# The first group's output projection, three of four head pairs: seven block products for eight

## The chip, the cores and the metric

The kernel runs on one core of a Trainium2 chip. The metric is the device time of one execution in microseconds. Several engines work side by side on a core and wait for one another through semaphores: TensorE (PE: matmuls; PEld is its loading of weights), VectorE (DVE), ScalarE (ACT), GpSimd (POOL); SyncE (SP) issues almost all transfers (DMA).

## What is computed

One layer of a decoder with two kinds of recurrent heads, for 2048 prompt tokens and 64 sample tokens at once. The part that matters here is the projection of the eight heads' outputs back to the model's width of 1024 and its addition to the residual:

```python
def mixer(h, pos, s_ret, s_hg, w_in, ...):
    proj = h @ w_in                          # 1024 -> 4096, cut into q, k, v, gates of 4 + 4 heads
    ...                                      # chunkwise recurrences, a norm per head, a swish gate
    o = jnp.concatenate([o_r, o_h], axis=-1) # 4 retention heads and 4 HGRN2 heads of 128
    return o @ w_out, s_ret_new, s_hg_new    # 1024 x 1024

xp = xp + mp                                 # mp: what mixer gave; the same for the samples
xp = xp + jnp.square(jax.nn.relu(rmsnorm(xp) @ w_up)) @ w_down
```

## The kernel before

**Tiling.** Tokens lie along the free dimension, features along the 128 partitions. They are cut into three groups (`GROUPS`) of 640, 768 and 704 tokens; the 64 samples are the first columns of the third, the rest are prompt tokens. For each group in turn the kernel makes the input norm (`norm_in`), the mixing (`mix`) and the output projection (`out_proj`); then for each group the feed forward (`ffn`), whose products are already made by a scheme of seven for eight.

**Numbers in two parts.** Every factor of a large product is split into `hi` (a rounded copy, made by ScalarE, L271 for weights and L349 for activations) and `lo` (the rest, made by VectorE, L285 and L350). A product is three matmuls: hi x hi, hi x lo, lo x hi. A matmul multiplies a 128 x 128 block of weights with at most 512 columns; a group of 640 tokens is done in two pieces of 320.

**Weights.** `w` lies in memory as tiles of 128 x 1024, eight blocks each, in the order of use. `plan_stream` writes that order; `weight` (L245) loads a tile through one of three `raw` buffers, and splits it into one of three `hi` and three `lo` buffers two tiles ahead of its use. The first group also stores the split parts of tiles 4 to 35 (`next_weight`, L319: 28 of the input projection and four of the output projection); the later groups load them back ("p" entries, L254) and split only the rest ("w"). Sums of weights for the feed forward are made beside the mixing of the second and third group by `plan_sums`, with four further buffers.

**Order.** The code is written in the order of TensorE's work. `tick` counts it: one tick for two matmuls of a projection. `later(n, f)` lets `f` emit its instructions n ticks on, so that side work is laid between matmuls. A scheduler then places the instructions on the engines' queues, in about the order in which they were emitted; each engine and SP work through their queues in order.

**Mixing.** Heads go in four pairs (one head of each kind). For each pair: the gates of the pair before, five projections, a long chain of recurrence work emitted by ticks (`mixer`), the values. After the fourth pair's values, `cut_heads` (L1178) splits the first three pairs' outputs at 2, 20 and 38 ticks, beside the last gates. The fourth pair's own chain ends later, beside the output projection, and `mixer` has its outputs cut then.

**Output projection.** `residual` (L1194) takes the eight output blocks in the order `N_ORDER`. For each it multiplies the six heads of three pairs (`proj`, L331; the matmuls are on L342): 6 x 3 x 2 = 36 matmuls, and adds the x block to the result out of PSUM (L1204). It uses six tiles of weights. After the second block `beside` starts `norm_in` of the next group at 12 ticks a piece: each of its eight pieces loads an x block into one of six `ld` buffers, and gives ScalarE two and VectorE two instructions (L546, L527, L547, L530). Then `out_proj` (L1240) waits until the fourth pair is cut, and adds its part for each block (12 matmuls, L1249), scales by the next norm's weight (L1250) and stores both (L1252). The last two tiles of weights belong to this.

## Time and profile before

| | |
|---|---|
| median of 3 runs | 2508.93 us (2508.18 to 2508.98) |
| the profiled execution, its own time | 2508.95 us |
| its span from the first to the last instruction | 2507.2 us |
| granted TensorE clock | 0.999 |
| first group's last gates begin | 273.5 us into the span |
| its projection of three pairs begins | 294.7 us |
| its fourth pair's part begins, ends | 348.1 us, 362.4 us |

Times within the profile count from the span's first instruction. "Busy" is time in which an engine executes; an engine can be busy less than the whole time and still be the one that others wait for in one stage. A line such as L1204 is that of the kernel's file; `out<-in` names the tiles written and read.

### The profile page before, as it was taken

To read this page: it belongs to the slowest core of one execution; us is meant where nothing else is said; L and a number is where in the kernel's file an instruction comes from. 1 tells how busy PE (TensorE), PEld (TensorE's weight loads), DVE (VectorE), ACT (ScalarE), POOL (GpSimd) and SP (SyncE) were. 2 spreads that over 40 slices of the span, in tenths; PEclk is the share of its full clock that TensorE was granted. 3 is DMA by queue.
4 is the path that set the end of the run, shared out by engine and by line. 5 is a ranking of instruction groups with operands and counts; after the bars stand their busy time and mean duration, and the time that the engine had idled before them with its cause. 6 is when DMAs were issued, how large, how long until landed. Compare 5 with 4: busy or idle time off the path is not lost.

```text
span 2507.2 us, 41510 instructions
## 1 busy us (share of the span) xinstructions
PE 2494.0 (99%) x16593; PEld 2474.9 (99%) x16593; DVE 1878.1 (75%) x2443; ACT 1253.9 (50%) x1674; POOL 366.1 (15%) x304
## 2 busy tenths in 40 slices
PE   9999999999999999999999999999999999999998
PEld 9999999999999999999999999999999999999998
DVE  7666865668684766677775899775699878678987
ACT  6665653444463444443644555444454436445544
POOL 5223304324411432340000000000000000000000
PEclk9999999999999999999999999999999999999999
DMA  7454563465575565758866856566675546867552
GB/s 269 164 185 168 209 225 135 160 228 185 199 244 212 194 215 195 264 206 306 305 216 213 284 198 213 173 237 221 202 261 177 189 148 202 274 192 247 192 187 88
DMA packets 189073, 525.39 MB, mean 210 GB/s; under 512 B 18640, under 2 KB 59856, under 8 KB 188880
## 3 DMA queue, kind: packets, MB, share of 16 engines
q1 hardware_dynamic: 188736, 522.73, 60.6%
q8 instruction: 130, 2.13, 0.3%
q14 instruction: 63, 0.52, 0.1%
q10 hardware_dynamic: 144, 0.02, 0.0%
HBM read 389.50 MB, written 132.38 MB: 208 GB/s over the span
## 4 chain that ended last, share of the span: by engine, by line
PE 96%; DVE 3%; ACT 1%; issue 1%; DMA 0%; DVEq 0%; ACTq 0%
PE pj L342 27%; PE pf L1189 26%; PE pj L1189 25%; PE pjv L732 8%; PE mm L898 1%; PE po L1078 1%; PE mm L1086 1%; PE po L1080 1%; PE mm L955 1%; PE mm L509 1%; PE mm L510 1%; PE mm L1012 1%; PE mm L830 0%; PE po L764 0%; DVE raw L1221 0%
## 5 line engine op out<-in xcount | busy, mean ns | idle before, releaser
L271 ACT CAST hi<-raw 128x1024 fp32r<-128x1024 f32 x392 | 413.1, 1054 | 610.0 <-PE pf L1189 261.4
L342 PE MATMUL pj<-slab,hi 128*128 128x320 f32 (+2 forms) x3072 | 661.5, 328 | 2.6 <-DVE slab L644 1.3
L1189 PE MATMUL pf<-slab,hi 128*128 128x320 f32 (+2 forms) x2768 | 659.1, 321 | 0.0
L1189 PE MATMUL pj<-slab,hi 128*128 128x352 f32 (+2 forms) x2608 | 622.1, 322 | 0.0
L285 DVE TENSOR_TENSOR lo<-raw,hi 128x1024 fp32r<-128x1024 f32 x392 | 485.3, 1238 | 111.9 <-ACT hi L271 105.8
L342 PEld LDWEIGHTS pj<-slab,hi 128*128 128x128 f32 x3072 | 508.1, 188 | 5.3 <-DVE slab L644 1.5
L1189 PEld LDWEIGHTS pf<-slab,hi 128*128 128x128 f32 x2768 | 481.9, 188 | 0.0
L1189 PEld LDWEIGHTS pj<-slab,hi 128*128 128x128 f32 x2608 | 454.5, 188 | 0.1
L1189 PE MATMUL pf<-slab,lo 128*128 128x320 f32 (+2 forms) x1384 | 445.5, 322 | 0.0
L1189 PE MATMUL pj<-slab,lo 128*128 128x352 f32 (+2 forms) x1304 | 420.3, 322 | 0.0
L342 PE MATMUL pj<-slab,lo 128*128 128x320 f32 (+2 forms) x1536 | 379.1, 328 | 0.4 <-DVE lo L285 0.4
L342 PEld LDWEIGHTS pj<-slab,lo 128*128 128x128 f32 x1536 | 263.3, 188 | 1.3 <-DVE lo L285 0.9
L1189 PEld LDWEIGHTS pf<-slab,lo 128*128 128x128 f32 x1384 | 260.3, 188 | 0.0
L1189 PEld LDWEIGHTS pj<-slab,lo 128*128 128x128 f32 x1304 | 245.3, 188 | 0.0
L732 PE MATMUL pjv<-hi,slab 128*128 128x256 f32 x1088 | 204.8, 285 | 0.0
L1280 ACT CAST slab<-slab 128x640 fp32r<-128x640 f32 (+2 forms) x192 | 145.7, 780 | 65.8 <-DVE slab L1291 52.2
L1284 DVE TENSOR_TENSOR slab<-slab 128x640 fp32r<-128x640 f32 (+2 forms) x192 | 167.3, 886 | 8.9 <-PE pj L1189 3.2
L732 PEld LDWEIGHTS pjv<-hi,slab 128*128 128x128 f32 x1088 | 172.2, 192 | 1.5 <-issue 0.2
L732 PE MATMUL pjv<-lo,slab 128*128 128x256 f32 x544 | 153.8, 283 | 0.0
L879 ACT ACTIVATE slab<-slab 128x640 f32<-128x640 f32 (+2 forms) x72 | 56.4, 784 | 154.6 <-POOL slab L875 154.4
L732 PEld LDWEIGHTS pjv<-lo,slab 128*128 128x128 f32 x544 | 104.2, 192 | 0.0
L1536 DVE TENSOR_TENSOR slab<-pf,slab 128x640 f32<-128x640 f32 (+2 forms) x88 | 77.6, 888 | 29.6 <-PE pf L1189 29.1
(218 smaller groups left out, 3004.1 us busy)
## 6 DMA issues: line engine op xcount, KB each, us to landing
raw<-w SPq DMA_DIRECT2D x264, 512.0 KB, 4.2
slab<-u SPq DMA_DIRECT2D x32, 384.0 KB, 4.7
u<-ld SPq DMA_DIRECT2D x30, 384.0 KB, 3.7
slab<-u SPq DMA_DIRECT2D x32, 352.0 KB, 4.5
u<-ld SPq DMA_DIRECT2D x30, 352.0 KB, 4.0
slab<-u SPq DMA_DIRECT2D x32, 320.0 KB, 4.5
u<-ld SPq DMA_DIRECT2D x30, 320.0 KB, 3.9
ld<-x SPq DMA_DIRECT2D x16, 384.0 KB, 3.6
```

The lines of the kernel that those rows point to most:

```text
L271: self.nc.scalar.copy(hi, raw)
L285: self.nc.vector.tensor_tensor(out=lo, in0=self.second.pop(j), in1=hi.bitcast(F32), op=ALU.subtract)
L342: self.nc.tensor.matmul(pj[:, i, :T2], w, a[:, c0:c1], start=j == 0 and q == 0, stop=j == n - 1 and q == 2)
L509: self.nc.tensor.matmul(ps, self.ones_r, hi, start=True, stop=False)
L510: self.nc.tensor.matmul(ps, self.ones_r, lo, start=False, stop=True)
L732: nc.tensor.matmul(pj[:, i * 256:(i + 1) * 256], a[:, s:s + C], ww, start=kb == 0 and q == 0, stop=kb == KB - 1 and q == 2)
L879: nc.scalar.activation(x["dd", w][:, a:T], x["dd", w][:, a:T], AF.Exp)
L898: nc.tensor.matmul(ps[:, j * P:(j + 1) * P], qk[:, cols[c]], qk[:, cols[c]], start=True, stop=True)
L1189: self.nc.tensor.matmul(*a, **k)
L1280: self.nc.scalar.copy(hi[:, :g.T], B[name][:, :g.T])
L1284: self.nc.vector.tensor_tensor(out=lo[:, :g.T], in0=B[name][:, :g.T], in1=hi.bitcast(F32)[:, :g.T], op=ALU.subtract)
L1536: nc.vector.tensor_tensor(out=r, in0=ps, in1=r, op=ALU.add)
```

## The change

For the first group alone (`OUT_SEVEN = (0,)`), the projection of the first three pairs is made by seven products for eight, in two quads t of four output blocks. In a quad the weights are a 2 x 2 arrangement A11, A12, A21, A22 (rows: the two halves of its four output blocks; columns: the HGRN2 and the retention heads), the activations B11, B12 (HGRN2 heads, first and second half of the tokens) and B21, B22 (retention heads). Sums S1 to S4 of weights and T1 to T4 of activations are multiplied, and the results added to four accumulators of a quad, and to a common term U that three of them get at the end.

* The order of the output projection's weights changes for all groups: eight tiles of 768 columns (one kind of head, two output blocks, three pairs), and two tiles of 1024 for the fourth pair. `N_OUT` goes from 8 to 10. `weight`, `second_part` and the kept copies handle the narrower tiles.
* `plan_sums` makes S1 to S4 for both quads beside the first group's mixing, starting at 400 and 592 ticks, and stores them; the products load them from there. A11 and A12 are the tiles that are kept for the later groups.
* `head_sums` replaces the three `cut_heads` of the first group: pairs 0 and 1 at 60 and 130 ticks of the fourth round of mixing, pair 2 beside the last gates.
* `out_seven` makes the 14 products in two PSUM buffers in turn. x is added to a quarter where its first product leaves PSUM. `norm_in` of the second group now starts after the sixth product, at 10 ticks a piece.
* `last_pair` adds the fourth pair by quarters.
* The second and third group's `residual` takes blocks in plain order, two tiles for two blocks.

The core of the diff:

```diff
-N_IN, N_OUT, N_UP, N_DN = 32, 8, 32, 32
+N_IN, N_OUT, N_UP, N_DN = 32, 10, 32, 32
-N_KEPT = W_OUT0 + 4
+WO = 2 * (H - 1) * P
-N_ORDER = (0, 1, 4, 5, 2, 3, 6, 7)
+OUT_SEVEN = (0,)
+OUT_PRODUCTS = ((0, "S4"), (0, "A11"), (1, "A11"), (0, "A12"), (1, "A12"), (1, "S4")) + tuple(
+    (t, name) for t in range(2) for name in ("S3", "S2", "A22", "S1"))
...
+        def mixing(g):
+            self.stream += [("p" if j >= N_MADE and g else "w", j, WT, j >= N_MADE and not g) for j in range(W_OUT0)]
+            products = OUT_PRODUCTS if g in OUT_SEVEN else [(t, name) for t in range(2) for name in ("A11", "A12", "A21", "A22")]
+            for t, name in products:
+                kept = name in ("A11", "A12")
+                e = entry(name, ("o", t), W_OUT0 + 4 * t, WO, kept and not g)
+                self.stream.append(("p",) + e[1:] if kept and g else e)
+            self.stream += [("w", W_UQ0 - 2 + j, WT, False) for j in range(2)]
...
+            self.plan_sums([(("o", t), W_OUT0 + 4 * t) for t in range(2)], [400, 592], WO)
             self.mix(gs[0])
-            self.out_proj(gs[0], 1, lambda: self.norm_in(gs[1], pace=12))
+            self.out_proj(gs[0], 1, lambda: self.norm_in(gs[1], pace=10))
...
+            if p == H - 1 and g.i in OUT_SEVEN:
+                g.ob = {name: [None] * (H - 1) for name in ("B11", "T1", "B21", "B22", "T2", "T3", "T4")}
+                for i in range(2):
+                    self.later(60 + 70 * i, self.head_sums, g, i)
...
+    def head_sums(self, g, p):
...
+        for d, fn, *a in ((0, keep, s, "B21", "B22"), (2, inner), (4, keep, o, "B11", "T1"), (8, outer),
+                          (11, keep, t, "T3", "T2"), (14, last)):
+            self.later(d, fn, *a)
...
+    def out_seven(self, g, beside):
...
+        def product(ps, op, first=True):
+            hi, lo = self.next_weight()
+            for i in range(2):
+                for p in range(H - 1):
+                    cols = slice((i * (H - 1) + p) * P, (i * (H - 1) + p + 1) * P)
...
+                    for j, (w, a) in enumerate(((hi, ah), (hi, al), (lo, ah))):
+                        self.matmul(ps[:, i], w[:, cols], a, start=first and p == 0 and j == 0,
+                                    stop=p == H - 2 and j == 2, skip_group_check=not first)
...
+        x(0, (0, 1))
+        x(0, (0, 0))
+        x(1, (0, 0))
+        x(1, (0, 1))
+        product(a, "B22")
+        new(0, (0, 1), a)
+        product(b, "B11")
+        for t, ps in ((0, b), (1, a)):
+            if t:
+                product(a, "B11")
+            acc[t]["U"] = self.get()
+            nc.scalar.copy(b2(acc[t]["U"]), ps)
+        for t, ps in ((0, b), (1, a)):
+            product(ps, "B21", False)
+            new(t, (0, 0), ps)
+            x(t, (1, 1))
+            x(t, (1, 0))
+        product(b, "B22")
+        new(1, (0, 1), b)
+        beside()
+        for t in range(2):
+            product(a, "T3")
+            new(t, (1, 1), a)
+            product(b, "T2")
+            add(acc[t]["U"], b, acc[t]["U"])
+            product(a, "T4", False)
+            new(t, (1, 0), a)
+            product(b, "T1")
+            add(acc[t][1, 1], b, acc[t][1, 1])
+            add(acc[t][0, 1], b, acc[t][0, 1])
+            for k, q in enumerate(((0, 1), (1, 1), (1, 0))):
+                self.later(4 + 8 * k, common, t, q)
...
     def residual(self, g, when, beside):
...
+        for m in range(KB // 2):
+            w = [self.next_weight(), self.next_weight()]
+            for i in range(2):
```

More of the change, by code (lines that the diff above doesn't have):

```diff
@@ L170, in lay_out_weights @@
     wo = w_out.reshape(2, H, P, KB, P)
-    for ps in (range(0, H - 1), range(H - 1, H)):
-        bl = [wo[kind, p, :, n] for n in N_ORDER for p in ps for kind in (1, 0)]
-        for j in range(0, len(bl), 8):
-            w[i] = np.stack(bl[j:j + 8], 1).reshape(P, WT)
+    for n in range(0, KB, 2):
+        for kind in (1, 0):
+            w[i, :, :WO] = wo[kind, :H - 1, :, n:n + 2].transpose(1, 2, 0, 3).reshape(P, WO)
+            w[i, :, WO:] = 0
             i += 1
+    for n in range(0, KB, 4):
+        w[i] = wo[::-1, H - 1, :, n:n + 4].transpose(1, 2, 0, 3).reshape(P, WT)
+        i += 1
     wu = w_up.reshape(2, KB // 2, P, NQ, 2, 2, P)
@@ L253, in weight @@
                 for part, kept in zip(self.wts[j], self.kept[e[1]]):
-                    self.nc.sync.dma_start(part.bitcast(F32), kept)
+                    self.nc.sync.dma_start(part[:, :e[2]].bitcast(F32), kept)
                 self.w_next += 1
@@ L257, in weight @@
                 continue
-            while self.w_load <= j or j >= W_UQ0 and self.w_load <= j + 2 and self.w_load < n:
+            while self.w_load <= j or j >= self.n_first and self.w_load <= j + 2 and self.w_load < n:
                 if self.stream[self.w_load][0] == "p":
@@ L265, in weight @@
                 e = self.stream[k]
-                self.fetch(raw, self.sums[e[1]] if e[0] == "s" else self.I["w"][e[1]])
+                self.fetch(raw[:, :e[2]], self.sums[e[1]] if e[0] == "s" else self.I["w"][e[1]][:, :e[2]])
                 self.w_load += 1
@@ L270, in weight @@
             lo = self.wp.tile([P, WT], F32R, tag="lo", name="lo")
-            self.nc.scalar.copy(hi, raw)
+            w = self.stream[j][2]
+            self.nc.scalar.copy(hi[:, :w], raw[:, :w])
             self.wts[j] = (hi, lo)
@@ L283, in second_part, with entry @@
         if j in self.second:
-            hi, lo = self.wts[j]
-            self.nc.vector.tensor_tensor(out=lo, in0=self.second.pop(j), in1=hi.bitcast(F32), op=ALU.subtract)
+            (hi, lo), w = self.wts[j], self.stream[j][2]
+            self.nc.vector.tensor_tensor(out=lo[:, :w], in0=self.second.pop(j)[:, :w], in1=hi[:, :w].bitcast(F32), op=ALU.subtract)
     def plan_stream(self):
-        self.stream = [("w", j) for j in range(W_UQ0)]
-        def entry(name, key, i0):
-            return ("s", key + (name,)) if name[0] == "S" else ("w", i0 + A_PLACE[name])
-        def mixing():
-            self.stream += [("p" if N_MADE <= j < N_KEPT else "w", j) for j in range(W_UQ0)]
+        self.stream = []
+        def entry(name, key, i0, cols=WT, keep=False):
+            return ("s", key + (name,), cols, False) if name[0] == "S" else ("w", i0 + A_PLACE[name], cols, keep)
+        def mixing(g):
[6 more added lines that the diff above has]
+            self.stream += [("w", W_UQ0 - 2 + j, WT, False) for j in range(2)]
         def feed_forward():
@@ L302, in feed_forward @@
                     self.stream += [entry(name, ("d", o, v), W_DQ0 + 4 * (2 * o + v)) for v in range(2)]
-        mixing()
-        mixing()
+        mixing(0)
+        self.n_first = len(self.stream)
+        mixing(1)
+        mixing(2)
         self.n_sums = len(self.stream)
@@ L315, in next_weight @@
         r = self.weight(i)
-        if N_MADE <= i < N_KEPT:
-            self.kept[i] = [self.dp.tile([P, WT], F32, name=f"w{i}{part}") for part in ("hi", "lo")]
-            for part, kept in zip(r, self.kept[i]):
-                self.nc.sync.dma_start(kept, part.bitcast(F32))
+        _, j, cols, keep = self.stream[i]
+        if keep:
+            self.kept[j] = [self.dp.tile([P, cols], F32, name=f"w{j}{part}") for part in ("hi", "lo")]
+            for part, kept in zip(r, self.kept[j]):
+                self.nc.sync.dma_start(kept, part[:, :cols].bitcast(F32))
         self.wts.pop(i - 4, None)
@@ L634, in mix @@
             prev = b
-        for p in range(H - 1):
-            self.later(2 + 18 * p, self.cut_heads, g, p)
+        if g.i in OUT_SEVEN:
+            self.later(2, self.head_sums, g, H - 2)
+        else:
+            for p in range(H - 1):
+                self.later(2 + 18 * p, self.cut_heads, g, p)
         self.gates(g, prev)
@@ L1192, in matmul, with keep, inner, outer @@
             self.tick()
+    def head_sums(self, g, p):
+        nc, T, T2 = self.nc, g.T, g.T // 2
+        o, s = g.o[p][1], g.o[p][0]
+        first, second = (lambda t: t[:, :T2]), (lambda t: t[:, T2:T])
+        t, t4 = self.get(), self.get()
+        sub = lambda out, a, b, op=ALU.subtract: nc.vector.tensor_tensor(out=out, in0=a, in1=b, op=op)
+        def keep(slab, *names):
+            hi, lo = self.getr(), self.getr()
+            self.cut(slab, hi, lo, T)
+            for name, half in zip(names, (first, second)):
+                g.ob[name][p] = (half(hi), half(lo))
+        def inner():
+            sub(first(t), second(s), second(o))
+            sub(second(o), second(o), first(o))
+        def outer():
+            sub(second(t), first(t), first(o), ALU.add)
+            sub(first(t4), first(s), second(t))
+        def last():
+            g.ob["T4"][p] = self.parts(first(t4), T2)
+        for d, fn, *a in ((0, keep, s, "B21", "B22"), (2, inner), (4, keep, o, "B11", "T1"), (8, outer),
+                          (11, keep, t, "T3", "T2"), (14, last)):
+            self.later(d, fn, *a)
@@ new lines, in rows, with x, add, common @@
+    def rows(self, g, name, n, c0, c1):
+        s = self.load()
+        o = KB * g.off
+        src = self.I["x"][:, o:o + KB * g.T].rearrange("p (k t) -> p k t", k=KB)
+        self.fetch(s[:, :2 * (c1 - c0)].rearrange("p (i t) -> p i t", i=2), src[:, n:n + 2, c0:c1])
+        return s
+    def out_seven(self, g, beside):
+        nc, T, T2 = self.nc, g.T, g.T // 2
+        b2 = lambda s: self.pair(g, s)
+        banks = [self.pj.tile([P, 2, 512], F32, tag="pj", name="pj")[:, :, :T2] for _ in range(2)]
+        g.banks = banks
+        acc, xs = [{}, {}], [{}, {}]
+        assert not self.blocks
+        def x(t, q):
+            xs[t][q] = self.rows(g, "x", 4 * t + 2 * q[0], q[1] * T2, (q[1] + 1) * T2)
+        def product(ps, op, first=True):
+            hi, lo = self.next_weight()
+            for i in range(2):
+                for p in range(H - 1):
+                    cols = slice((i * (H - 1) + p) * P, (i * (H - 1) + p + 1) * P)
+                    if g.ob[op][p] is None:
+                        while g.ob[op][p] is None:
+                            self.tick()
+                    ah, al = g.ob[op][p]
+                    for j, (w, a) in enumerate(((hi, ah), (hi, al), (lo, ah))):
+                        self.matmul(ps[:, i], w[:, cols], a, start=first and p == 0 and j == 0,
+                                    stop=p == H - 2 and j == 2, skip_group_check=not first)
+        def add(out, ps, s):
+            nc.vector.tensor_tensor(out=b2(out), in0=ps, in1=b2(s), op=ALU.add)
+        def common(t, q):
+            nc.vector.tensor_tensor(out=acc[t][q][:, :T], in0=acc[t][q][:, :T], in1=acc[t]["U"][:, :T], op=ALU.add)
+        def new(t, q, ps):
+            acc[t][q] = self.get()
+            add(acc[t][q], ps, xs[t].pop(q))
+        a, b = banks
+        x(0, (0, 1))
[30 more added lines that the diff above has]
+                self.later(4 + 8 * k, common, t, q)
+        g.ob = None
+        while H - 1 not in g.oc:
+            self.tick()
+        return acc
@@ new lines, in last_pair @@
+    def last_pair(self, g, acc):
+        nc, T, T2 = self.nc, g.T, g.T // 2
+        k = 0
+        for t in range(2):
+            for row in range(2):
+                n, blocks = 4 * t + 2 * row, self.take(4)
+                for h in range(2):
+                    ps = g.banks[k % 2]
+                    k += 1
+                    for i in range(2):
+                        for j in range(2):
+                            (wh, wl), (ah, al) = blocks[2 * i + j], g.oc[H - 1][j]
+                            for q, (w, a) in enumerate(((wh, ah), (wh, al), (wl, ah))):
+                                self.matmul(ps[:, i], w, a[:, h * T2:(h + 1) * T2], start=j == q == 0, stop=j == 1 and q == 2)
+                    r, b = acc[t][row, h], self.get()
+                    nc.vector.tensor_tensor(out=self.pair(g, r), in0=ps, in1=self.pair(g, r), op=ALU.add)
+                    for i in range(2):
+                        nc.scalar.activation(self.pair(g, b)[:, i], self.pair(g, r)[:, i], AF.Copy,
+                                             scale=self.vec[:, V_FFN + n + i:V_FFN + n + i + 1])
+                    for kept, s in ((g.res, r), (g.in_, b)):
+                        nc.sync.dma_start(kept[:, n:n + 2, h * T2:(h + 1) * T2], self.pair(g, s))
@@ L1194, in residual @@
     def residual(self, g, when, beside):
-        acts = [a for p in range(H - 1) for a in g.oc[p]]
+        acts = [g.oc[p][j] for j in range(2) for p in range(H - 1)]
         part = {}
-        for j, n in enumerate(N_ORDER):
-            if j == when:
-                beside()
-            x = self.x_block(g, n)
-            pj = self.proj(g, self.take(2 * (H - 1)), acts)
-            part[n] = self.get()
-            self.nc.vector.tensor_tensor(out=self.v2(part[n], g), in0=pj, in1=self.v2(x, g), op=ALU.add)
+        assert not self.blocks
@@ new lines, in residual @@
+        for m in range(KB // 2):
+            w = [self.next_weight(), self.next_weight()]
+            for i in range(2):
+                n = 2 * m + i
+                if n == when:
+                    beside()
+                x = self.x_block(g, n)
+                blocks = [tuple(s[:, c * P:(c + 1) * P] for s in w[j]) for j in range(2) for c in range(i * (H - 1), (i + 1) * (H - 1))]
+                pj = self.proj(g, blocks, acts)
+                part[n] = self.get()
+                self.nc.vector.tensor_tensor(out=self.v2(part[n], g), in0=pj, in1=self.v2(x, g), op=ALU.add)
@@ L1207, in residual, with plan_sums @@
         return part
-    def plan_sums(self, sets, starts):
+    def plan_sums(self, sets, starts, cols=WT):
         nc, w = self.nc, self.I["w"]
@@ L1216, in load @@
             for name in names:
-                x[name] = self.wp.tile([P, WT], F32, tag="sum", name="raw", bufs=4)
-                self.tc.keep_in_program_order(nc.sync.dma_start(x[name], w[i + A_PLACE[name]]))
+                x[name] = self.wp.tile([P, WT], F32, tag="sum", name="raw", bufs=4)[:, :cols]
+                self.tc.keep_in_program_order(nc.sync.dma_start(x[name], w[i + A_PLACE[name]][:, :cols]))
         def make(x, name, a, op, b, into):
@@ L1224, in keep @@
         def keep(x, key, name):
-            s = self.sums[key + (name,)] = self.dp.tile([P, WT], F32, name="s" + "".join(map(str, key)) + name)
+            s = self.sums[key + (name,)] = self.dp.tile([P, cols], F32, name="s" + "".join(map(str, key)) + name)
             self.tc.keep_in_program_order(nc.sync.dma_start(s, x[name]))
@@ L1242, in out_proj @@
         nc, T = self.nc, g.T
+        g.res, g.in_ = (self.dp.tile([P, KB, T], F32, name=f"{name}{g.i}") for name in ("res", "in"))
+        if g.i in OUT_SEVEN:
+            acc = self.out_seven(g, beside)
+            between()
+            self.last_pair(g, acc)
+            self.flush()
+            return
         part = self.residual(g, when, beside)
         between()
-        g.res, g.in_ = (self.dp.tile([P, KB, T], F32, name=f"{name}{g.i}") for name in ("res", "in"))
-        for n in N_ORDER:
+        for n in range(KB):
             pj = self.proj(g, self.take(2), g.oc[H - 1])
```

## The prediction

> **What bounds the kernel now.** I read the page first, then the busy time by stage around the first group's output projection, the groups of instructions there, and the order of VectorE's work in it.

> ```profile
> span 2507.2 us, 41510 instructions
> ...
> PE 2494.0 (99%) x16593; PEld 2474.9 (99%) x16593; DVE 1878.1 (75%) x2443; ACT 1253.9 (50%) x1674; POOL 366.1 (15%) x304
> ...
> PE 96%; DVE 3%; ACT 1%; issue 1%; DMA 0%; DVEq 0%; ACTq 0%
> ```

> TensorE is busy for 99% of the span and carries 96% of the chain that ended last. The waits of TensorE, over the whole span, show that almost nothing can be won by removing stalls; the three longest lines of that view:

> ```profile
> PE pj L342 <- DVE slab L644: 1.3, 1, 1.3
> PE mm L409 <- DVE eps L413: 1.1, 1, 1.1
> PE pj L342 <- ACT hi L271: 0.7, 1, 0.7
> ```

> So removed matmuls are worth their full time, as long as the engines that feed TensorE keep up. Whether they do is read from the stage itself. The windows below cut the first group's projection after 108, 252 and 288 matmuls of L342, and end after the last 96 (the fourth pair). Columns are start and end, length, then busy time and count of PE, PEld, DVE, ACT, POOL, the granted clock, the DMA share and GB/s. The last row is a hundred microseconds of feed forward, where products by seven already run.

> ```profile
> 294.68:316.35 21.67, 21.47 (x158) 21.20 (x157) 19.45 (x39) 16.05 (x22) 1.57 (x1) 1.00 0.63 215
> 316.35:341.32 24.97, 24.97 (x179) 24.97 (x177) 22.73 (x35) 17.92 (x28) 0.00 (x0) 1.00 0.63 200
> 341.32:348.12 6.80, 6.80 (x49) 6.59 (x48) 1.54 (x4) 1.97 (x5) 1.89 (x2) 1.00 0.49 174
> 348.12:362.42 14.30, 14.30 (x99) 14.07 (x97) 9.47 (x10) 7.59 (x9) 1.77 (x1) 1.00 0.83 291
> 1400.00:1500.00 100.00, 100.00 (x684) 100.00 (x683) 94.95 (x112) 52.81 (x65) 0.00 (x0) 1.00 0.68 233
> ```

> The reader should see two things. VectorE at 90% (19.45 of 21.67 us, 22.73 of 24.97) or even 95% (94.95 of 100) does not hold TensorE up; and this stage is already at 90%, far above the kernel's mean of 75%, because the next group's input norm (L547, L530) is laid beside it.

> **What is removed.** The chain of waits has a stretch of nothing but these matmuls:

> ```profile
> 329.44 14.38 PE pj L342 x98
> ```

> That is 14.38 / 98 = 146.7 ns for one of 320 columns. Before, three pairs take 8 blocks x 6 inputs x 3 parts x 2 pieces = 288 of them; after, 2 quads x 7 products x 2 x 3 x 3 = 252, of the same width. The 36 that go are worth 36 x 146.7 ns = 5.28 us, the most the change can bring. The fourth pair's 96 stay, and so does the mixing work of that pair that TensorE does in between (it is tied to ticks of two matmuls, not to the blocks). The profiled execution took 2508.95 us (2507.2 of span and 1.75 around it), like the median of 2508.93; 0.2% of it, what a measurement of this kernel can tell from no change, is 5.0 us. So the whole gain would only just count as faster.

> **What is added beside it.** VectorE's instructions in the projection, and seven starts in a row that give what one costs when they queue (start to next start, shorter than the duration because they overlap):

> ```profile
> L285 DVE TENSOR_TENSOR lo<-raw,hi 128x1024 fp32r<-128x1024 f32 x8 | 10.4, 1302 | 0.4 <-ACT hi L271 0.3
> L547 DVE SCALAR_TENSOR_TENSOR slab<-ld,vec,slab 128x768 fp32r<-128x768 f32 x8 | 8.1, 1014 | 0.5 <-ACT slab L546 0.3
> L530 DVE TENSOR_TENSOR slab<-slab 128x768 f32<-128x768 f32 x7 | 6.7, 953 | 0.1
> L1204 DVE TENSOR_TENSOR slab<-pj,ld 128x640 f32<-128x640 f32 x8 | 6.6, 819 | 0.4 <-PE pj L342 0.4
> L885 DVE TENSOR_TENSOR slab<-slab 128x320 f32<-128x320 f32 x1 | 0.5, 493 | 0.0
> ```

> ```profile
> 334.14 0.83 DVE L350 TENSOR_TENSOR slab<-slab 128x640 fp32r<-128x640 f32 x1
> 334.88 1.22 DVE L285 TENSOR_TENSOR lo<-raw,hi 128x1024 fp32r<-128x1024 f32 x1
> 336.02 0.82 DVE L350 TENSOR_TENSOR slab<-slab 128x640 fp32r<-128x640 f32 x1
> 336.75 1.01 DVE L547 SCALAR_TENSOR_TENSOR slab<-ld,vec,slab 128x768 fp32r<-128x768 f32 x1
> 337.68 0.95 DVE L530 TENSOR_TENSOR slab<-slab 128x768 f32<-128x768 f32 x1
> 338.55 0.81 DVE L1204 TENSOR_TENSOR slab<-pj,ld 128x640 f32<-128x640 f32 x1
> 339.29 1.01 DVE L504 TENSOR_TENSOR slab<-slab 128x384 fp32r<-128x384 f32 x2
> ```

> A second part of 1024 columns costs 336.02 - 334.88 = 1.14 us, a 640-wide operation 0.74 (334.88 - 334.14, and 339.29 - 338.55 for one that reads PSUM), a 768-wide one 0.87 (338.55 - 337.68), the norm's first one 0.93; a norm piece is 1.80. The changed tiles are 768 wide: I take 0.87 for their second parts.

> *First six products (54 ticks, 108 matmuls, still 21.67 us of TensorE).* VectorE has 19.45 us now. Out go three second parts (3.4), two additions (1.5) and the norm's three and two (4.5), since `beside` is called only after the sixth product: 10.0 us are left, the fourth pair's mixing. In come six second parts (5.2) and three additions (2.2). 17.5 of 21.67 us: covered.

> *The other eight products and the fourth pair.* TensorE's time is 24.97 + 6.80 + 14.30 - 5.28 = 40.79 us. VectorE has 22.73 + 1.54 + 9.47 = 33.74 us now. Second parts: six of 768 and four of 1024 (9.8) for five (5.7), +4.1. Additions: 11 out of PSUM and 6 of the common term for 6 of L1204, +11 x 0.74 = +8.1. All eight norm pieces now fall here, at a pace of 10 ticks: 8 x 0.93 + 7 x 0.87 = 13.5 for 9.0, +4.5. Together 33.74 + 16.7 = 50.4 us of work for 40.79 us of cover, 9.6 us too much. The work is in one queue in about program order: the norm's piece of a tick stands ahead of the next product's second part and of the addition that empties its bank. There are two banks in turn, so a product waits once the addition two products back is late; TensorE then runs at VectorE's pace.

> How much of the 9.6 us TensorE loses: at the end, the last addition (0.74) and a second part for the next group (1.14) may lag, which leaves 7.7. The 4.2 us that VectorE has free in the first stretch help little: the six load buffers take the first six of the eight x quarters at once and the other two as they come free, so the first row of the norm can be loaded only after the fifth product. The same buffers delay the pieces, and the last may fall behind the fourth pair's additions, into the next mixing:

> ```profile
> 362.42:380.00 17.58, 17.58 (x104) 17.58 (x103) 5.54 (x6) 7.64 (x8) 1.40 (x1) 1.00 0.58 206
> ```

> There VectorE is busy for only 5.54 of 17.58 us. Lower bound: nothing, if the square sums (7 x 0.87 = 6.1 us) and one more of the norm's operations slip there; upper bound: VectorE reaches no more than the 95% of the feed-forward row, 50.4 / 0.95 = 53.0, so 7.7 + 2.6 = 10.3. I take one piece of 1.8 us that falls behind: 7.7 - 1.8 = 5.9 us, between the ends and nearer to the tally of this stage.

> [...]

> *Beside the first mixing.* Head sums of pairs 0 and 1 now fall into the fourth round: three second parts of 640 (2.2), four half-width sums and one half cut (at most 0.5 each by L885) are some 4.5 us of VectorE for a pair, and one of the two weight sets adds 4 x 0.87 = 3.5. The round before its last gates:

> ```profile
> 213.00:273.45 60.45, 60.45 (x455) 60.24 (x455) 39.65 (x72) 37.72 (x53) 16.39 (x15) 1.00 0.47 167
> ```

> 39.65 + 12.5 = 52.2 of 60.45 us, 86%: under the 95% that did no harm, so nothing. Without that cover it would cost at most the 12.5 us. The third pair's sums take the place of three pairs' cuts in the last gates (six second parts of 640 then; three, a half one and four half-width sums now), no more than before. The 16 new transfers of the weight sums (384 KB each) go through SP where the DMA share is 0.47.

> *Weights of the groups after.* Their two tiles of a pair of blocks are now held together, with three buffers of hi and of lo. The second tile of the next pair gets its buffer only when the first of this pair is done, 18 matmuls before the pair's end, and is needed 18 into the next: 36 matmuls of cover, 5.3 us at 320 columns (more at 384 and 352), where one tile lay ready ahead before. In the second group's projection (issue to landing, and SP's waits):

> ```profile
> hi<-w34hi SPq DMA_DIRECT2D x1, 512.0 KB, 3.6
> raw<-w SPq DMA_DIRECT2D x9, 512.0 KB, 4.3
> SPq L234 <- DVE slab L547: 8.8, 4, 4.3
> ```

> A reload of 3.6 us fits; one that is queued in SP behind an x load that waits 4.3 us for a buffer doesn't (7.9 us). Bounds: nothing, and for three such tiles in each of two groups 6 x (7.9 - 5.3) = 16 us; I take 1.0, near the lower end, as only one of the four waits can be expected to fall there. TensorE's work of these groups is unchanged.

> **Sum.** 2508.95 - 5.28 + 5.9 + 0 + 1.0 = 2510.6 us: the gain is eaten by VectorE in the same stage.

> **Rivals.**
> - *The whole gain.* The norm's pieces slip behind the products, and VectorE's low load after the projection takes them. For it: VectorE's four windows leave 14.6 us free, and the load buffers do delay the pieces. Against: VectorE's work of the whole projection would be 17.5 + 50.4 = 67.9 us for 62.5 of TensorE. 2508.95 - 5.28 = 2503.7. [...] Chance 0.17, of which 0.13 beyond 0.2%.
> - *Slower, by VectorE's queue.* No norm piece falls behind and VectorE stays at 95%: 10.3 us are lost, 2508.95 - 5.28 + 10.3 + 1.0 = 2515.0. It decides from 10.3 us of waits in all, where the sum passes 0.2%. For it: pieces are emitted ahead of the additions that they delay. Against: the norm's rows come late. Chance 0.20.
> - *Slower, by the weights of later groups.* The reload waits in SP more often than not: half of the six tiles, 8 us, with the 5.9 of the forecast: 2517.6. It decides where a second tile lands over 5.3 us after its buffer is free. Chance 0.10.

> The forecast keeps 0.53. **How the numbers follow.** Faster 0.13; slower 0.20 + 0.10 = 0.30; within 0.2% 0.53 + 0.04 = 0.57. The range goes from 2504.2, inside the whole gain, to 2518.0, past both slower cases; what is left out is the better half of the first rival and the worst of the last.

> **What would show it.** Right: 36 fewer matmuls, a projection about as long as now (67.7 us, where 62.5 would be the whole gain), TensorE's waits for VectorE's second parts and additions in its second half some 6 us in place of none, VectorE at 95% or more there. Wrong: TensorE full in that stretch with the norm's pieces after it; or waits of L342 for reloads in the second and third projection; or new waits in the fourth round of the first mixing, which I put at nothing.

## The result: slower by 0.85%, and the profile after

| | before | after |
|---|---|---|
| median | 2508.80 us (2508.18 to 2508.98) | 2529.64 us (2529.29 to 2531.71) |
| ratio | | 1.0085 [1.0073, 1.0098] |
| span of the profiled execution | 2507.2 us | 2529.9 us |

The change costs 20.8 us. The profiled execution is the slowest of its kernel's four (2531.71 us), so the spans differ by 22.7. The page of the kernel after, its span, its busy times and the engines of the chain that ended last:

```profile
span 2529.9 us, 41588 instructions
PE 2497.7 (99%) x16557; PEld 2474.7 (98%) x16557; DVE 1908.5 (75%) x2493; ACT 1262.1 (50%) x1702; POOL 365.9 (14%) x304
PE 85%; DVE 2%; ACT 0%; issue 0%; DVEq 0%; ACTq 0%
```

The 36 matmuls are gone (16,593 to 16,557), yet TensorE is busy for longer: 2497.7 us for 2494.0. By the matmuls alone it should be 5.3 us less, and it is 3.7 more; the granted clock gives up to an estimated 6.8 of these 9.0 us (below). The waits of TensorE over the whole span (us in total, times, longest), the six longest:

```profile
PE pj L1215 <- DVE slab L1283: 9.5, 6, 2.3
PE pj L1215 <- DVE slab L670: 3.1, 1, 3.1
PE mm L529 <- DVE slab L368: 2.5, 2, 2.3
PE mm L981 <- DVE AT L968: 2.2, 1, 2.2
PE mm L924 <- DVE slab L912: 1.2, 2, 0.6
PE mm L528 <- ACT slab L367: 1.2, 1, 1.2
```

Before, the longest was 1.3 us. L1215 holds the matmuls of the products, L1283 is the addition that empties their PSUM buffer (PSUM is where matmuls leave their results, `pj` and `mm` in the rows; the other tiles lie in SBUF), L670 the operation that empties the last gate's; L981, L924, L528 and L529 belong to the recurrence of a pair and its norm (the 2.3 of L529 is in the third group). Five of six lines name VectorE. By stage, cut at TensorE's own instructions as in the prediction (last gates, first six products, the other eight, the fourth pair):

```profile
274.36:302.36 28.00, 23.72 (x163) 21.61 (x163) 20.47 (x28) 11.33 (x23) 12.70 (x11) 0.94 0.38 137
302.36:329.70 27.34, 22.53 (x162) 21.76 (x161) 20.72 (x44) 17.01 (x24) 1.55 (x1) 1.00 0.62 202
329.70:364.20 34.50, 27.32 (x178) 25.89 (x176) 33.27 (x47) 25.91 (x38) 0.00 (x0) 0.95 0.67 214
364.20:383.90 19.70, 17.33 (x105) 16.76 (x106) 15.61 (x21) 11.03 (x23) 3.67 (x2) 0.91 0.89 308
```

| stage, us | before | less 36 matmuls | after | lost |
|---|---|---|---|---|
| up to the last gates | 273.5 | 273.5 | 274.4 | 0.9 |
| last gates | 21.2 | 21.2 | 28.1 | 6.9 |
| first six products | 21.7 | 21.7 | 27.2 | 5.5 |
| the other eight | 31.8 | 26.5 | 34.5 | 8.0 |
| fourth pair | 14.2 | 14.2 | 19.7 | 5.5 |
| all that follows | 2144.9 | 2144.9 | 2146.0 | 1.1 |

All but 2 us lie in 110 us around the changed projection. In the third row VectorE is busy for 33.27 of 34.50 us: 96%, and TensorE for 27.32. How the queue makes TensorE wait shows in VectorE's order of work there, from the timeline of the kernel after (start, length, engine):

```profile
340.52 0.81 DVE L1283 TENSOR_TENSOR slab<-pj,slab 128x640 f32<-128x640 f32 x1
341.26 1.01 DVE L566 SCALAR_TENSOR_TENSOR slab<-ld,vec,slab 128x768 fp32r<-128x768 f32 x1
342.18 0.95 DVE L293 TENSOR_TENSOR lo<-raw,hi 128x768 fp32r<-128x768 f32 x1
343.12 0.96 DVE L549 TENSOR_TENSOR slab<-slab 128x768 f32<-128x768 f32 x1
344.00 0.55 DVE L1200 TENSOR_TENSOR slab<-slab 128x384 f32<-128x384 f32 x1
344.47 0.82 DVE L1283 TENSOR_TENSOR slab<-pj,ld 128x640 f32<-128x640 f32 x1
...
345.34 0.56 PE L1215 MATMUL pj<-slab,hi 128*128 128x320 f32 x2 [1.04 <-DVE slab L1283]
```

Between two additions that empty PSUM stand a norm piece (L566, L549), a second part of weights (L293) and the fourth pair's work (L1200): 3.2 us of work, and 3.95 us from the start of one addition to that of the next, where the 18 matmuls of a product take 2.64 (18 x 146.7 ns). The next product starts 0.05 us after the second addition ends.

**The clock.** Ahead of the last 30 us of the span, TensorE's granted clock falls to one half four times, each for 3.413 us: from 284.4, 356.1, 369.7 and 1147.9 us. The row of the first stretch in the kernel after, with 14 matmuls of 320 columns or less in 3.42 us:

```profile
284.40:287.82 3.42, 3.42 (x14) 3.42 (x14) 0.82 (x1) 0.46 (x2) 0.00 (x0) 0.51 0.87 275
```

Before has none there. A stretch costs up to 1.7 us: an estimate, half of its 3.413 us. With it the loss adds up. The gaps of over 0.3 us between weight loads (PEld, one load to a matmul) are 7.1 us in all before and 29.5 after: -5.3 + 22.4 + 4 x 1.7 = 23.9 us against 22.7 more span (parts of the stretches lie on waits). The same sum comes close for kernels below: in light_vector -5.3 + (22.3 - 7.1) + 2 x 1.7 = 13.3 for 13.3 measured, in all_three_out -5.3 + (13.2 - 7.1) + 1.7 = 2.5 for 3.0.

### The profile page after: what moved, and what is told of

The parts are those of the page before. It is cut to its first block, busy times and chain, and to the rows that moved or that the text cites. A ratio compares the mean times of both kernels' runs of the same rounds, so it can differ in the third digit from the quotient of the medians.

```text
span 2529.9 us, 41588 instructions
## 1 busy us (share of the span) xinstructions
PE 2497.7 (99%) x16557; PEld 2474.7 (98%) x16557; DVE 1908.5 (75%) x2493; ACT 1262.1 (50%) x1702; POOL 365.9 (14%) x304
## 4 chain that ended last, share of the span: by engine, by line
PE 85%; DVE 2%; ACT 0%; issue 0%; DVEq 0%; ACTq 0%
PE pf L1215 26%; PE pj L1215 26%; PE pj L360 20%; PE pjv L758 6%; PE mm L924 1%; PE mm L1112 1%; PE po L1104 1%; PE po L1106 1%; PE mm L981 1%; PE mm L529 1%; PE mm L528 1%; PE po L790 0%; PE mm L1038 0%; PE mm L856 0%; PE pj L1535 0%
## 5 line engine op out<-in xcount | busy, mean ns | idle before, releaser
L279 ACT CAST hi<-raw 128x1024 fp32r<-128x1024 f32 (+1 forms) x404 | 419.5, 1038 | 639.4 <-PE pf L1215 254.5
L1215 PE MATMUL pj<-slab,hi 128*128 128x320 f32 (+2 forms) x2840 | 677.5, 322 | 13.2 <-DVE slab L1283 9.5
L1215 PE MATMUL pf<-slab,hi 128*128 128x320 f32 (+2 forms) x2768 | 659.0, 321 | 0.0
L360 PE MATMUL pj<-slab,hi 128*128 128x352 f32 (+2 forms) x2816 | 614.7, 331 | 1.0 <-ACT hi L279 1.0
L293 DVE TENSOR_TENSOR lo<-raw,hi 128x1024 fp32r<-128x1024 f32 (+1 forms) x404 | 494.3, 1223 | 123.3 <-ACT hi L279 110.9
L1215 PEld LDWEIGHTS pj<-slab,hi 128*128 128x128 f32 x2840 | 494.4, 189 | 15.7 <-DVE slab L1283 3.9
L1215 PEld LDWEIGHTS pf<-slab,hi 128*128 128x128 f32 x2768 | 481.7, 188 | 0.0
L360 PEld LDWEIGHTS pj<-slab,hi 128*128 128x128 f32 x2816 | 470.1, 189 | 3.6 <-ACT hi L279 1.2
L1215 PE MATMUL pj<-slab,lo 128*128 128x320 f32 (+2 forms) x1420 | 457.5, 322 | 0.0
L1215 PE MATMUL pf<-slab,lo 128*128 128x320 f32 (+2 forms) x1384 | 445.5, 322 | 0.0
L360 PE MATMUL pj<-slab,lo 128*128 128x352 f32 (+2 forms) x1408 | 350.4, 330 | 0.6 <-DVE lo L293 0.4
L1215 PEld LDWEIGHTS pj<-slab,lo 128*128 128x128 f32 x1420 | 268.0, 189 | 0.0
L1215 PEld LDWEIGHTS pf<-slab,lo 128*128 128x128 f32 x1384 | 260.2, 188 | 0.0
L360 PEld LDWEIGHTS pj<-slab,lo 128*128 128x128 f32 x1408 | 242.9, 189 | 1.5 <-DVE lo L293 1.1
L1706 DVE TENSOR_TENSOR slab<-pf,slab 128x640 f32<-128x640 f32 (+2 forms) x88 | 77.5, 886 | 29.5 <-PE pf L1215 28.9
## 6 DMA issues: line engine op xcount, KB each, us to landing
raw<-w SPq DMA_DIRECT2D x254, 512.0 KB, 4.4
```

What stands on the lines that cost most here:

```text
L279: self.nc.scalar.copy(hi[:, :w], raw[:, :w])
L293: self.nc.vector.tensor_tensor(out=lo[:, :w], in0=self.second.pop(j)[:, :w], in1=hi[:, :w].bitcast(F32), op=ALU.subtract)
L360: self.nc.tensor.matmul(pj[:, i, :T2], w, a[:, c0:c1], start=j == 0 and q == 0, stop=j == n - 1 and q == 2)
L1215: self.nc.tensor.matmul(*a, **k)
L1706: nc.vector.tensor_tensor(out=r, in0=ps, in1=r, op=ALU.add)
```

## The experiments

My theory: VectorE's queue is overfull from the last gates to the fourth pair. Rivals for parts of the loss: the pool of 44 slabs, in which the sums of heads stay far longer than the outputs that they replace; the sums of weights beside the mixing; the narrower tiles by themselves. Stages are in us, found as in the table above; a statement's line number can be up to ten higher, or one lower, in a variant. "Half clock" counts stretches of 3.41 us before the last 30 us of the span.

| kernel | median | gates | first six | other eight | fourth pair | span | half clock |
|---|---|---|---|---|---|---|---|
| before | 2508.8 | 21.2 | 21.7 | 31.8 | 14.2 | 2507.2 | 0 |
| after | 2529.6 | 28.1 | 27.2 | 34.5 | 19.7 | 2529.9 | 4 |
| layout_only | 2511.8 | 21.2 | 23.1 | 31.7 | 14.7 | 2511.3 | 1 |
| hold_ten_slabs | 2513.9 | 25.4 | 21.9 | 32.5 | 14.2 | 2512.4 | 0 |
| shared_slabs | 2527.3 | 26.9 | 22.8 | 34.5 | 20.6 | 2524.4 | 4 |
| no_weight_sums | 2530.5 | 24.3 | 27.2 | 34.5 | 19.5 | 2525.6 | 3 |
| sums_early | 2529.8 | 24.3 | 27.2 | 36.0 | 20.3 | 2528.5 | 4 |
| work_moved | 2531.6 | 29.2 | 27.2 | 36.6 | 21.6 | 2534.5 | 8 |
| light_vector | 2522.3 | 26.6 | 27.2 | 27.6 | 19.2 | 2520.5 | 2 |
| squares_on_gpsimd | 2534.8 | 27.9 | 27.2 | 37.0 | 21.2 | 2533.1 | 7 |
| norm_spread | 2527.7 | 28.1 | 27.2 | 29.4 | 20.0 | 2526.3 | 2 |
| all_three_out | 2511.7 | 21.2 | 23.4 | 27.6 | 17.8 | 2510.2 | 1 |
| one_addition_less | 2510.6 | 21.2 | 23.4 | 27.5 | 17.1 | 2508.8 | 1 |

**layout_only**: the new tiles and order of weights, with the old products. The next group's norm starts where it does in the kernel before, which is after the first block (`j == when` with `when` 1), not after the second.

```diff
-OUT_SEVEN = (0,)
+OUT_SEVEN = ()
-            self.plan_sums([(("o", t), W_OUT0 + 4 * t) for t in range(2)], [400, 592], WO)
-            self.out_proj(gs[0], 1, lambda: self.norm_in(gs[1], pace=10))
+            self.out_proj(gs[0], 1, lambda: self.norm_in(gs[1], pace=12))
```

> The change without products by seven: weights of the output projection in the new tiles and order, no weight sums, no head sums, the next norm after the first block at 12 ticks as before. If what is lost after the first group (1.2 us in the profile: a wait of 2.5 us and half a clock for 3.4 us in the third group's projection) comes from the new tiles, this loses 1 to 3 us: 2510 to 2512. If it only comes from where the first group left the queues, it equals the kernel before, 2508.8 within 0.7.

2511.82 us, ratio 1.0013 [1.0004, 1.0022]: the tiles cost some 3 us by themselves. Its longest wait, in the view of TensorE's waits:

```profile
PE mm L528 <- DVE slab L368: 3.5, 2, 2.3
```

One of the two waits, 1.1 us, ends at 308.8, in the projection, the other, 2.3, at 1128.9, in the third group's mixing, with a stretch of half clock behind it. No line of this view names a reload. So the loss of the later groups (1.3 us from the first group's end on) is there, but it isn't the reloads that I had priced.

**hold_ten_slabs**: the kernel before, with ten slabs held from the fourth round until the third pair is cut, and only one-column operations of GpSimd on them.

```diff
+            if p == H - 1 and g.i == 0:
+                g.held = []
+                for i in range(2):
+                    self.later(60 + 70 * i, self.hold, g)
...
+    def hold(self, g):
+        for _ in range(5):
+            s = self.get()
+            self.nc.gpsimd.memset(s[:, :1], 0.0)
+            g.held.append(s)
```

> The kernel before, with ten slabs taken and held without work: five from tick 60 and five from tick 130 of the first group's fourth round, let go when the third pair has been cut (a one-column fill and a one-column sum on GpSimd each). Theory of the slabs: the pool of 44 is full then, the fourth pair's recurrence is emitted late and in a bunch, and TensorE waits in the last gates and at the start of the projection: 5 to 13 us more, 2514 to 2522. Theory of the work (VectorE, ScalarE and SP have too much to do with the sums): no slab is worked on, so 2509 within 1.

2513.91 us, 1.0021 [1.0012, 1.0031]: 5.3 us more, at the foot of what the theory of the slabs expected. Holding slabs alone makes the gates 4.2 us longer. The two longest lines of TensorE's waits, where the kernel before has one wait of 1.3 in place of the first line and none like the second:

```profile
PE pj L342 <- DVE slab L654: 2.3, 2, 1.3
PE mm L908 <- DVE slab L896: 2.0, 2, 1.3
```

The wait for a slab can be seen. GpSimd's first operation of a part of the fourth pair's recurrence (`exponents`; L874 in the kernel before, L884 here, L900 in the kernel after) takes a fresh slab, and its input is long made. When it waits for an instruction whose result it doesn't read, it waits for a slab to come free. From the waits around the last gates, the kernel before, this one and the kernel after:

```profile
POOL slab L874 <- PE pj L342: 2.9, 1, 2.9
```

```profile
POOL slab L884 <- DVE slab L350: 5.3, 1, 5.3
```

```profile
POOL slab L900 <- PE pj L360: 12.6, 2, 9.1
```

In the built programs, L360 and L350 are there the last to read what the slab held before. The operations on ScalarE, VectorE and TensorE that follow (in this kernel L889, L896, L908) wait in turn.

**shared_slabs**: the sums of pair 1 are written over those of pair 0, and the products read them for both; the instructions are the same, seven slabs fewer are held.

```diff
-            hi, lo = self.getr(), self.getr()
+            hi, lo = g.same[names] if p == 1 else (self.getr(), self.getr())
+            if p == 0:
+                g.same[names] = hi, lo
```

> The changed kernel, with the sums and cuts of pair 1's heads written into the slabs of pair 0's (the same instructions, seven slabs fewer; the products of pair 1 then read what is there). Theory of the slabs: the waits in the last gates and at the start of the projection go for the most part, and half a clock with them: 6 to 12 us less, 2518 to 2524. Theory of the work: the work is all there, so 2529.6 within 1.

2527.34 us, 1.0077 [1.0062, 1.0092], between the two expectations. The first six products fall from 27.2 to 22.8: the wait of 3.1 us for L670 is gone. That was the emptying of the last gate's PSUM buffer, which came only at 308.55 us, 6 us after the gate's end, and held the second product. The gates themselves gain little (26.9 for 28.1): TensorE waits there once for 4.0 us (L982 for L985), and the pool still fills up to 44.

**no_weight_sums** and **sums_early**: the sums of weights left out, or made in the first two rounds.

```diff
+            if key[0] == "o" and name[0] == "S":
+                return "w", i0 + A_PLACE[("A21", "A22")[int(name[1]) % 2]], cols, False
...
-            self.plan_sums([(("o", t), W_OUT0 + 4 * t) for t in range(2)], [400, 592], WO)
```

```diff
-            self.plan_sums([(("o", t), W_OUT0 + 4 * t) for t in range(2)], [400, 592], WO)
+            self.plan_sums([(("o", t), W_OUT0 + 4 * t) for t in range(2)], [16, 208], WO)
```

> Leaves out the making of the sums of weights: products S1 to S4 read plain tiles of weights instead, so that eight sums on VectorE, their eight stores and their eight first loads are gone; the products load as much as before. If the weight sums are what delays VectorE beside the last gates: the gates fall from 28.1 to 21 to 23 us, and the first six products from 27.2 towards 23; time 2518 to 2524. If it is the slabs and the head sums: the gates stay above 26 and the time at 2526 to 2530.

> The whole computation; the sums of weights are planned at ticks 16 and 208 of the mixing (first and second round) in place of 400 and 592. If the weight sums beside the last gates cause the stall there: gates 21 to 24 us, time 2520 to 2525. If the slabs do it: gates stay at 27 to 28, time 2527 to 2531. If VectorE has as little room in the first rounds: those rounds grow by up to 7 us and the time does not fall.

Both bring the gates to 24.3 us: the wait of 2.2 us for L968 and the half clock behind it are gone. The first six products stay at 27.2, and without the sums the second half stays as it is too. The medians, 2530.50 (2527.69 to 2531.52) and 2529.84 (2528.91 to 2530.89), aren't lower than after's, which neither expectation had: the 3.8 us show in the stage and not in the time. The profile of no_weight_sums is that of its fastest execution, at a mean clock of 0.997; the two slowest show 0.994, so more half clock there fits the lost gain. With the sums early, the time up to the fourth round grew by 2.0 us, and the second half by 2.1.

**work_moved**: weight sums at 150 and 342 ticks, head sums at 120 and 164 for 60 and 130.

```diff
-                    self.later(60 + 70 * i, self.head_sums, g, i)
+                    self.later(120 + 44 * i, self.head_sums, g, i)
```

> The whole computation; the sums of weights are planned at ticks 150 and 342 in place of 400 and 592, and the sums of heads of pairs 0 and 1 at 120 and 164 ticks of the fourth round in place of 60 and 130, so that their slabs are held for a shorter time. Expected from the runs with weight sums out (gates 24.3) and with seven slabs fewer (first six products 22.8): gates 22 to 25, first six products 23 to 26; the second half stays at 34.5 and 19.7, as VectorE has no less to do there; time 2521 to 2526. If VectorE's work only moves from one stage to the next, gates and first six products gain less than 3 together: 2527 to 2531.

2531.57 us (2529.72 to 2536.30). The expectation fell: the gates grew to 29.2, and the first six products stayed at 27.2. Holding the slabs for a shorter time doesn't help where the pool is at its fullest, in the last gates: the built program has 43 to 44 slabs in use there, as the kernel after has. The gates hold the same four head sums (L1226) as in the kernel after, one cut (L368) more and one more each of L911, L912 and L523: VectorE has 21.64 us of work there for 20.61, though the weight sums' 1.9 are gone from it.

**light_vector**: 11.5 us of VectorE's work left out of the second half.

```diff
-            for k, q in enumerate(((0, 1), (1, 1), (1, 0))):
-                self.later(4 + 8 * k, common, t, q)
...
-                g.sq = self.add_square(g, g.sq, x, nc.vector)
+                sq = self.add_square(g, None if g.i == 1 else g.sq, x, nc.vector)
+                g.sq = g.sq if g.i == 1 and kb else sq
```

> Leaves out part of the computation: the six additions of the common term U, and seven of the eight additions of squares of the second group's norm (ScalarE still makes the squares). That is 6 x 0.81 + 7 x 0.95 = 11.5 us of VectorE work between the sixth product and the end of the fourth pair; nothing else changes. If VectorE's queue is what the eight products and the fourth pair wait for: the eight products fall from 34.5 to 27 to 29 us, the fourth pair from 19.7 to 15 to 17, and the time from 2529.6 to 2516 to 2521. If the waits come from buffers, PSUM or weights: not below 2526. The gates (28.1) and the first six products (27.2) stay as they are by both.

2522.34 us, 1.0056 [1.0039, 1.0072]. Its windows of the eight products and the fourth pair:

```profile
327.57:355.13 27.56, 25.64 (x178) 24.91 (x177) 25.91 (x38) 23.47 (x36) 0.00 (x0) 1.00 0.76 244
355.13:374.40 19.27, 17.16 (x105) 16.89 (x106) 12.90 (x17) 13.16 (x25) 3.66 (x2) 0.91 0.96 343
```

The eight products fall by 6.9 us, as VectorE does by 7.4 (33.27 to 25.91): in that stage its queue is the bound. The fourth pair didn't follow (19.2 for 15 to 17 expected), and the time stayed 1.3 us above the expected range: a wait of 2.1 us for L1284 early in the fourth pair and the half clock after it are left.

**squares_on_gpsimd**: seven additions of squares given to GpSimd.

```diff
-                g.sq = self.add_square(g, g.sq, x, nc.vector)
+                g.sq = self.add_square(g, g.sq, x, nc.gpsimd if g.i == 1 else nc.vector)
```

> The changed kernel, with the seven sums of squares of the second group's input norm on GpSimd in place of VectorE. Theory of VectorE's queue in the last eight products: 7 x 0.87 = 6.1 us leave the queue, so its waits there fall by some 6 of 10.7 us, and half clocks may go with them: 2520 to 2524. Rival, the weights (loading, hi, second part through three buffers in 2.6 us a product) set the pace: 2529.6 within 1.5.

2534.82 us, 1.0103 [1.0088, 1.0118]: slower, which neither expectation had, with the eight products at 37.0. The timelines of GpSimd and of VectorE in it:

```profile
342.36 1.86 POOL L549 TENSOR_TENSOR slab<-slab 128x768 f32<-128x768 f32 x1 [4.11 <-ACT slab L546]
344.81 1.92 POOL L549 TENSOR_TENSOR slab<-slab 128x768 f32<-128x768 f32 x1 [0.59 <-ACT slab L546]
```

```profile
340.27 0.94 DVE L293 TENSOR_TENSOR lo<-raw,hi 128x768 fp32r<-128x768 f32 x1
...
342.06 0.81 DVE L1283 TENSOR_TENSOR slab<-pj,ld 128x640 f32<-128x640 f32 x1
342.80 2.24 DVE L293 TENSOR_TENSOR lo<-raw,hi 128x768 fp32r<-128x768 f32 x1
344.96 2.18 DVE L1200 TENSOR_TENSOR slab<-slab 128x384 f32<-128x384 f32 x1
...
348.73 0.54 DVE L1200 TENSOR_TENSOR slab<-slab 128x384 f32<-128x384 f32 x1
```

The same instruction takes 0.94 us alone and 2.24 beside GpSimd's addition, another 0.54 and 2.18. So the 0.95 us that an addition saves VectorE is given back by the instruction that runs beside it, 1.30 and 1.64 us longer here. L1283, which reads PSUM, keeps its 0.81 us beside GpSimd (342.06). TensorE's longest wait here, 4.1 us, is for the fourth pair's cut (L367), which waits for the last L1200 of this list. L293 and L1200, which read two tiles in SBUF, end 0.82 and 0.41 us after the GpSimd addition beside them does, close to the 0.94 and 0.54 that they take alone: in these two rows it is as if they had run only once it was done. What makes them wait, no run shows.

**norm_spread**: the second group's norm at 16 ticks a piece for 10.

```diff
-            self.out_proj(gs[0], 1, lambda: self.norm_in(gs[1], pace=10))
+            self.out_proj(gs[0], 1, lambda: self.norm_in(gs[1], pace=16))
```

> The whole computation; the second group's norm is laid at 16 ticks a piece in place of 10, so that its pieces reach into the fourth pair. VectorE's work between the sixth product and the end of the fourth pair stays what it is, only bunched less. If the sum of the queue's work decides: the eight products get 3 to 5 us shorter (34.5 to about 30), the fourth pair as much longer, time 2527 to 2531. If only the bunching at 10 ticks does it: time 2520 to 2525, with the fourth pair at 20 us or less.

2527.65 us, 1.0076 [1.0059, 1.0093]. The eight products lose 5.1 us of their 34.5, the fourth pair stays at 20.0. But the gaps of the two stages together are 10.0 us for 10.7 after: the waits have only moved, as the sum of the queue's work says (here and under the prediction, a gap is the time between two starts of matmuls less 0.147 us, counted from 0.3 us up). What was won are the two stretches of half clock that after has there; they did not occur here.

**all_three_out**: light_vector, no_weight_sums and shared_slabs in one; **one_addition_less**: also without the second addition that the last product of the second quad needs.

```diff
-            add(acc[t][0, 1], b, acc[t][0, 1])
+            if t == 0:
+                add(acc[t][0, 1], b, acc[t][0, 1])
```

> Leaves out all three: the weight sums, the common additions and the sums of squares, and the sums of two pairs of heads lie in the same slabs (seven slabs fewer). The matmuls are those of the changed kernel. If VectorE's queue and the slabs are the whole of it: gates 21 to 22, first six products 22 to 23, the other eight 26.5 to 28, fourth pair 14 to 16; time 2505 to 2510. If something else holds the products, such as the two PSUM buffers or the narrower tiles: above 2514.

> As all_three_out, and without one more part: the second quad's last product is added to one accumulator only, not to two, so that its PSUM buffer is free one addition of 0.82 us earlier. If the last wait that all_three_out has ahead of the fourth pair (2.25 us) is that product's two additions in a row: it falls by 0.7 to 0.9 to 1.4 to 1.5, and the time by 0.5 to 1.5, from 2511.7 to 2510.2 to 2511.2. If the wait is for a weight or an activation: no change in it.

2511.69 us, 1.0013 [1.0004, 1.0022], and 2510.61 us, 1.0009 [1.0000, 1.0018]. The waits of TensorE from the gates to the fourth pair, first of all_three_out, then of one_addition_less:

```profile
PE pj L1218 <- DVE slab L1293: 3.9, 3, 2.1
PE mm L529 <- ACT slab L369: 1.2, 1, 1.2
```

```profile
PE pj L1218 <- DVE slab L1293: 3.2, 3, 1.4
PE mm L529 <- ACT slab L369: 1.2, 1, 1.2
```

The gates are back at 21.2, the eight products within 1.1 us of their 26.5. The first time is above the 2505 to 2510 expected, the fourth pair above its 14 to 16. Three causes, with three of the four stretches of half clock, cover 18 of the 21 us. Of the rest, one wait is part of the design: the last product's buffer is read by two additions in a row, and the fourth pair's products, of 12 matmuls each, don't cover that; one addition less makes this wait 0.7 us shorter (2.1 to 1.4) and the median 1.1 lower, though single runs of the two overlap. The 1.2 us in the first six products and a wait of 2.4 in the third group stand where layout_only has its two.

## Why the prediction was wrong

The forecast was 2510.6 us, the time is 2529.6. Of the 21 us of span beyond the forecast, 12.4 were lost in the gates and the first six products, which it put at nothing, and 7.6 are the second half beyond its 5.9.

- *Removed*: right. 36 matmuls, 5.3 us; the balances of gaps above close with it.
- *"Beside the first mixing ... so nothing"*: the step that failed most. I compared VectorE's work with the round's length (86%) and did not count slabs. In the built program's order of instructions, 43 to 44 of 44 are in use in the first half of the last gates, where the kernel before needs 34 to 41. Ten slabs held in the kernel before cost the gates 4.2 us; seven fewer give the first six products 4.4 back; without the weight sums the gates gain 3.8. With all out both stages return, but for 1.7 us. This term was 0; gates and first six products lost 12.4, a stretch of half clock among it. I also put the third pair's sums at "no more than before" and the first six products at "covered": their 17.5 us of VectorE would have been, but work that was late in the gates came in front (20.72 us), the last gate's emptying among it. GpSimd's waits for slabs, 12.6 us in the gates for 2.9 before, show some of this lateness; what each of them delayed was not tried piece by piece. In the gates VectorE also stood still for 4.1 us ahead of a second part whose buffer TensorE, at half clock for the first 2.4 of them, still used.
- *VectorE in the other eight products and the fourth pair*: the mechanism was right, by the prediction's own words ("a product waits once the addition two products back is late"), and the size was not. I took 5.9 of 0 to 10.3, on the guess that a norm piece would fall behind. None did: the gaps in these two stages are 10.7 us, and VectorE is at 96% in the eight products, so the upper bound of 10.3 was the value. The tally of the work held: 33.27 + 15.61 = 48.9 us busy for 50.4. Half clock added some 2.7, which makes 13.4.
- *Weights of later groups*: 1.0, and 1.3 was lost in layout_only, but by VectorE's queue in the third group and the clock behind it, not by reloads: the number was right by luck. Why the narrower tiles make that queue later stays open.
- *The clock*: no term at all. Waits were priced at their own length, while TensorE's clock is halved after some of them, four times here, for up to 6.8 us by the estimate above.
- *The rivals*: "slower, by VectorE's queue" was the right one for the second half and too cheap, 2515.0 for 2529.6, since it had neither the slabs nor the clock. That a lighter second half alone would do falls too: light_vector is still 13.5 us above before.

## What to carry to other kernels

A scheme that saves matmuls pays in sums. Add up the vector engine's work over the whole stretch in which it can't be moved away, and where that is more than the matmuls' time, take the upper bound, which held here. Count the buffers that live longer, at their fullest point, beside the work. And price a wait of TensorE of two microseconds at more than its length: here one of 1.86 us or more within a window of the clock (below) cost up to an estimated 1.7 more.

## What the hardware showed

```profile
283.20:287.30 4.10, 4.01 (x36) 4.00 (x37) 0.86 (x2) 1.31 (x4) 0.00 (x0) 1.00 0.88 290
```

That is 36 matmuls in 4.10 us after the wait, where after has 14 in 3.42. The grid's place differs from run to run (the clock first came up 4.48 us into the span of the kernel after, 5.09 in that of the kernel before), which fits the wider scatter of these kernels (2.4 us over after's four runs, 0.8 over before's). What sets the grid, no run shows.
